# Neighbouring columns for the extra blocks of layer 0's experts, one layout of the down weights, and one order of stages for the later experts

## The chip, the cores and the metric

The kernel is one program on one core of a Trainium2 chip. Its engines are TensorE (PE in the rows: matmuls; PEld: its weight loads), VectorE (DVE), ScalarE (ACT), GpSimd (POOL) and SyncE (SP, which here only issues transfers); sixteen DMA engines move data between HBM and the on-chip memory SBUF. The metric is the device time of one execution in microseconds (us). Lower is better.

## The reference

Two layers of a diffusion backbone run over 256 latent and 256 context tokens of width 1024 in float32. Each layer has a mixer (attention and a bidirectional recurrence) and then a mixture of 16 experts, of which each token uses two:

```python
def grouped_moe(h, router_w, router_b, w_gate, w_up, w_down):
    ...  # scores, two experts of one group for each token: combine (tokens x experts)
    out = jnp.zeros_like(h)
    for e in range(N_EXPERTS):
        hid = jax.nn.silu(h @ w_gate[e]) * (h @ w_up[e])
        out = out + combine[:, e:e + 1] * (hid @ w_down[e])
    return out
```

`w_gate` and `w_up` of an expert are 1024x512, `w_down` is 512x1024: 2 MB each, 6 MB an expert, 96 MB a layer. Layer 0 sends all 512 tokens through its experts, layer 1 only the 256 latent ones, and a final normalisation ends the kernel.

## The kernel before

The change lies in the experts of layer 0, in `experts`. Layer 1 has its own code (`experts_last`), which the diff leaves alone except that it shares `part`.

For each expert the tokens routed to it are gathered into slots: a main block of 64 slots, always computed, and up to three extra blocks of 32 slots (`NX = (3, 0)`), each of which runs only if the expert has so many tokens. The test is a branch at run time (`extras`, whose conditions show as L1594 in the profile).

An expert e runs through these stages:

- `gathers(e)`: POOL fetches the tokens' rows from HBM; `xtranses(e)`: PE transposes them, ScalarE copies the result.
- `up_stage(e)`: PE multiplies with gate and up (`up0`, 8 steps over k for the main block, gate and up side by side on 64 columns of the array each). For an extra block `upx` does the same in four groups of 32 columns of the array (2 matrices x 2 halves of the 512 hidden columns), each a matmul of 256 columns. Then Silu on ScalarE (L1473, its name kept in `mark`) and the product on VectorE (`hid0`, L1474; `hidx`, L1548, for the extra blocks).
- `htranses(e)`: PE transposes the hidden values, ScalarE copies them.
- `down_stage(e)`: PE multiplies with the down weights (`down0`, `downx`).
- `out_stage(e)`: VectorE weighs the rows (L1509) and POOL adds them to HBM by an indirect transfer that accumulates (`scatter`, L1449). Scatters of different experts wait for each other.

A matmul in float32 appears as two records in the trace. In the rows `ccg` is the result of `upx`, `ccd` that of `downx`, `pgu` that of `up0`, `pdn` that of `down0`, `phd` that of the turn of the main block's hidden values.

The loop over e is written out by hand (`manual_schedule`): the engines run in the order of the code. For experts 1 to 10 one turn of the loop does up(e+1), then down(e), then the turn of the hidden values of e+1, then the output of e. For expert 0 and for experts 11 to 14 (`late`) the turn does down(e) and the output of e first, then up(e+1), then the turn of e+1. Expert 15 has only its down and output left.

Weights. `part` gives a chunk of SBUF and the source of one of an expert's three matrices. A partition p holds rows p*k_count + k of the matrix ("(p k) n"), one run of 16 KB in HBM for each partition. So for down, partition p holds the hidden columns 4p to 4p+3, and the hidden values must be put in that order: `hid0` writes its product in a turned order, and `upx` reads the weight columns four apart. Eight chunks go round. `load_expert(l, e + 2)` is called at the start of turn e, and SyncE issues its transfers; from e = 4 on they wait for `mark[e]`, the Silu of expert e (line 215). Experts 13 and 14 come in four cuts of gate and up (512 KB each). Expert 15 comes through `last_loads`: a first pair of pieces waits for `mark[13]`, two more pairs for `mark[14]`, the last pair and the down weights in four pieces for `mark2[14]`, the weighing of expert 14's output.

Behind all this in SyncE's queue stands the load of layer 1's tokens from `yd`, which waits for the last scatter.

Of the kernel before, what the change touches and what calls it, by code (L numbers as in the profile page):

```python
# [17 lines left out]
OP = mybir.AluOpType  # L18
# [4 lines left out]
KC = D // P  # L23
# [3 lines left out]
NE = 16  # L27
# [81 lines left out]
def backbone(ctx: ExitStack, tc: tile.TileContext, a: dict):  # L109
    nc = tc.nc  # L110
    pe, act, dve, pool = nc.tensor, nc.scalar, nc.vector, nc.gpsimd

    def mm(out, lhsT, rhs, start, stop):
        pe.matmul(out, lhsT, rhs, start=start, stop=stop)  # L114
# [55 lines left out]
    def wchunk(name, pl=None, dt=F32):  # L170
        if pl is None:
            pl = wpool
        else:
            return pl.tile([P, 4096], dt, name=name, tag="w")
        if wx["pool"] is not None:
            if wx["only"] is None:
                i = wx["i"] % 8
                pl = wpool if i < 4 else wx["first"] if i < 4 + wx["nf"] else wx["pool"]
                wx["i"] += 1
            else:  # L180
                pl = wx["only"]
        return pl.tile([P, 4096], dt, name=name, tag="w")
# [26 lines left out]
    def part(l, e, i, pl=None):  # L209
        n_, k = (("gate", 8), ("up", 8), ("down", 4))[i]  # L210
        t = wchunk(f"w{n_[0]}{l}_{e}", pl).rearrange("p (k n) -> p k n", k=k)
        return t, a[f"exp_w_{n_}"][l, e].rearrange("(p k) n -> p k n", k=k)

    def load(t, src, after=None, q=nc.sync):
        d = q.dma_start(t, src)
        if after:
            tc.add_manual_dep(d.ins, after, mybir.DependencyInfo(mybir.DependencyClass.Sync, mybir.DependencyReason.DATA), reason="short queue")

    def load_part(l, e, i, q, after=None):
        t, src = part(l, e, i)  # L220
        load(t, src, after, q)
        return t

    def load_expert(l, e, cuts=(), after=None):


        if not cuts:
            return [load_part(l, e, i, nc.sync, after) for i in range(3)]
        ps = [part(l, e, i) for i in range(3)]
        for lo, hi in zip((0,) + cuts, cuts + (KC,)):  # L230
            for t, src in ps[0:2]:
                load(t[:, lo:hi, :], src[:, lo:hi, :], after)
        load(*ps[2], after)
        return [t for t, _ in ps]

    def last_loads(l, e):

        ps = [part(l, e, i) for i in range(3)]

        def rows(i, lo, hi, after):  # L240
            t, src = ps[i]
            load(t[:, lo:hi, :], src[:, lo:hi, :], after)

        def steps():
            for k in range(0, KC, 2):
                after = yield
                for i in range(2):
                    rows(i, k, k + 2, after)
            for k in range(4):
                after = yield  # L250
                rows(2, 4 // 4 * k, 4 // 4 * (k + 1), after)
        g = steps()
        next(g)
        return [t for t, _ in ps], g

    ada_w = [load_ada_part(0, 0, 2 * h, 2, wchunk(f"ada{h}"), h == 3) for h in range(4)]
    csil = const.tile([P, KC, 32], F32, name="csil")
# [19 lines left out]
    with tc.tile_pool(name="spt", bufs=1, reuse_waits="tile") as sp:  # L277
# [5 lines left out]
        t = sp.tile([P, 16], F32, name="st")  # L283
        act.activation(t[:], ab[:], AF.Exp, scale=-1.0)
        s = sp.tile([P, 16], F32, name="ss")
# [26 lines left out]
    rows = {}  # L312
# [1119 lines left out]
    def experts(l, tmp):  # L1432
        r = rt_all[l]
        nt, n = r["nt"], r["n"]
        rk, ci, oi = r["rk"], r["ci"], r["oi"]
        nx = r["nx"]
        xg0, xgx, cps = (bk[n_] for n_ in ("xg0", "xgx", "cps"))
# [32 lines left out]
        def hid0(ps):  # L1470
            t = tmp.tile([P, 4, P], F32, name="hid", tag="hid", bufs=1)
            sg, h = t[64:128].rearrange("s k p -> s (k p)"), t[0:64]
            mark.append(act.activation(sg, ps[0:64, :], AF.Silu).ins.name)  # L1473
            dve.tensor_tensor(h.rearrange("s k p -> s p k"), sg.rearrange("s (p k) -> s p k", k=4),  # L1474
                              ps[64:128, :].rearrange("s (p k) -> s p k", k=4), op=OP.mult)
            return h

        def htrans0(h):
# [29 lines left out]
        def weigh(y, ps, w):  # L1508
            return dve.scalar_tensor_tensor(y, ps, w, y, op0=OP.mult, op1=OP.mult)  # L1509
# [24 lines left out]
        def upx(b, x, w):  # L1534
            for k in range(8):
                sx = x[:, b, k % 2, 32 * (k // 2):32 * (k // 2) + 32]
                for m in range(2):
                    for q in range(2):
                        wv = w[m][:, k, :].rearrange("p (c i) -> p i c", i=4)[:, 2 * q:2 * q + 2, :]
                        o = cps["cg"][64 * m + 32 * q:64 * m + 32 * q + 32, b, :].rearrange("p (i c) -> p i c", i=2)  # L1540
                        mm(o, sx, wv, k == 0, k == 7)

        def hidx():
            ps = cps["cg"]
# [56 lines left out]
        PEe, Pe = mybir.EngineType.PE, mybir.EngineType.Pool  # L1601
        W = {}
        mark = []
        mark2 = []
        oh = {}

        def onehot(e):
            if e < NE:
                oh[e] = one_hot(l, tmp, nx, rk[:, :, e])

        def infos(e):
            if e < NE:
                info[e] = slot_info(l, tmp, e, nx, oh.pop(e))
# [7 lines left out]
        def xtranses(e):  # L1621
            if e < NE:
                xt[e] = xtrans0(xg0[e % NG]), xtransx(e % NG)
# [19 lines left out]
        def out_stage(e, pd, y0, yx):  # L1643
            gs, w, _ = info[e]
            scats.clear()
            mark2.append(weigh(y0, pd, w[:, 0:1]).ins.name)
            scatter(y0, gs[:, 0:1], yd[l][:])
            for b in range(nx):
                weigh(yx[:, b, :], cps["cd"][:, b, :], w[:, 1 + b:2 + b])
            extras(Pe, e, lambda b: scatter(yx[:, b, :], gs[:, 1 + b:2 + b], ydx))  # L1650

        W[0] = load_expert(l, 0)
        with tc.manual_schedule(engines=ORDERED):
            W[1] = [load_part(l, 1, 0, nc.sync), wx["w"][0][0]]
            wx["i"] += 1
            onehot(0)
            infos(0)
            warm(ident, 8)
            r["counts"](tmp)
            gathers(0)  # L1660
            W[1].append(load_part(l, 1, 2, nc.gpsimd))
            onehot(1)
            infos(1)
            gathers(1)
            W[2] = [load_part(l, 2, i, nc.gpsimd if i < 2 else nc.sync) for i in range(3)]
            onehot(2)
            xtranses(0)
            infos(2)
            gathers(2)
            gates2()  # L1670
            onehot(3)
            up_stage(0)
            infos(3)
            xtranses(1)
            gathers(3)
            onehot(4)
            htranses(0)
            up_stage(1)
            infos(4)

            ahead_g = {0: (4,), 1: (5,), 2: (6,), 3: (7,), 4: (8,), 5: (9, 10)}
            ahead_i = {0: (5,), 1: (6,), 2: (7,), 3: (8,), 4: (9, 10)}
            for e in range(NE):
                if e + 2 < NE and e:
                    if e + 2 < NE - 1:
                        W[e + 2] = load_expert(l, e + 2, (2, 4, 6) if e + 2 >= 13 else (), mark[e] if e >= 4 else None)
                    else:
                        W[e + 2], more = last_loads(l, e + 2)
                        for _ in range(1):
                            more.send(mark[e])  # L1690
                late = e == 0 or 11 <= e < NE - 1
                if late:
                    pd = down_stage(e)
                    out_stage(e, pd, pick0(e, info[e][2]), pickx(e, info[e][2]))
                    if e == NE - 2:
                        for i in range(5):
                            try:
                                more.send(mark2[e])
                            except StopIteration:
                                break  # L1700
                xtranses(e + 2)
                for i in ahead_g.get(e, (e + 5,)):
                    gathers(i)
                for i in ahead_i.get(e, (e + 6,)):
                    onehot(i)
                    if e and i == ahead_i.get(e, (i,))[-1]:
                        up_stage(e + 1)
                        if e + 1 == NE - 2:
                            for _ in range(2):
                                more.send(mark[e + 1])  # L1710
                    infos(i)
                if late:
                    htranses(e + 1)
                    continue
                pd = down_stage(e)
                ys = pick0(e, info[e][2]), pickx(e, info[e][2])
                htranses(e + 1)
                out_stage(e, pd, *ys)
# [5 lines left out]
        with tc.If(anyv > 0, preferred_fallthrough_block=False):  # L1724
            for e in range(NE):
                ov = nc.values_load(oi[0:1, e:e + 1], min_val=0, max_val=8)
                with tc.If(ov > 0, preferred_fallthrough_block=False):
                    w = load_expert(l, e)
                    dve.memset(base[:], float(NB + 32 * nx))
                    with tc.For_i(0, ov, 1):  # L1730
# [5 lines left out]
                        ps = psb("pgu", "mm")  # L1736
                        up0(ps, x, w)
                        h = htrans0(hid0(ps))
                        ps = psb("pdn", "mm")
# [323 lines left out]
```

## Time and profile before

| | |
|---|---|
| median of 3 runs | 1153.78 us (1147.43 to 1154.68) |
| the profiled execution | 1154.09 us |
| its span from the first to the last instruction | 1152.3 us |
| mean granted TensorE clock in it | 0.936 of full speed |
| TensorE matmuls busy | 1020.5 us, 89% of the span |
| VectorE / ScalarE / GpSimd busy | 604.0 / 432.0 / 194.6 us |
| HBM read and written | 288.86 and 10.49 MB, 260 GB/s over the span |

The times of the rows are from the profiled execution and count from the start of its span. Busy time is that of an engine's own instructions; matmuls are pipelined and their ends are modelled, so the starts are the better guide to their rate. Where a row names the end of an idle time ("<-"), that is the releaser as inferred from semaphores.

### The profile page before, as it was taken

Reading aid. Unit: us, or ns where it says so; the run is one execution under the profiler, and the core shown is the slowest. Engines: PE = TensorE matmul, PEld = TensorE weight load, DVE = VectorE, ACT = ScalarE, POOL = GpSimd, SP = SyncE. Lnnn points to the kernel's source line nnn. Section 1 sums busy time; section 2 is a strip of 40 time slices with the busy share of each in tenths; the row PEclk is TensorE's granted clock in tenths of the full one; section 3 lists DMA queues with packets and bytes.
Section 4 is the critical chain, followed back from the end, with each engine's and each line's share of the span. In section 5 each row is a group of like instructions: output and inputs, shape, how many; then the busy total and the mean of one; then the engine's idle time right before and its main releaser. Section 6 shows DMA issues by size and latency. Waiting matters only on the chain. (4 is left out here: it accounts for less than half of the span.)

```text
span 1152.3 us, 15548 instructions
## 1 busy us (share of the span) xinstructions
PE 1020.5 (89%) x5791; PEld 526.3 (46%) x5791; DVE 604.0 (52%) x1363; ACT 432.0 (37%) x858; POOL 194.6 (17%) x208
## 2 busy tenths in 40 slices
PE   5999998999499998999987759997997899999993
PEld 3655555777333433333333246443676444344431
DVE  3567477787612224454443236579966144444445
ACT  3635776565311111221222054677753121122222
POOL 2100052412542211320210020102432000000000
PEclk9999999899599898999999779988997999999996
DMA  9956682103566656999995484548418699999951
GB/s 375 371 213 258 229 306 99 62 4 141 244 243 236 198 221 206 371 412 397 396 400 182 159 280 185 187 155 305 161 47 354 241 403 411 431 403 416 413 220 40
DMA packets 46252, 298.90 MB, mean 259 GB/s; under 512 B 5504, under 2 KB 8448, under 8 KB 28336
## 3 DMA queue, kind: packets, MB, share of 16 engines
q1 hardware_dynamic: 39472, 279.88, 61.5%
q0 software_dynamic: 6512, 16.87, 5.1%
q8 instruction: 74, 1.21, 0.4%
q10 hardware_dynamic: 144, 0.52, 0.1%
q14 instruction: 50, 0.41, 0.1%
HBM read 288.86 MB, written 10.49 MB: 260 GB/s over the span
## 5 line engine op out<-in xcount | busy, mean ns | idle before, releaser
L114 PE MATMUL pdn<-wd,hidT 128*64 128x512 f32 x512 | 129.6, 642 | 0.5 <-PEq L1594 0.4
L114 PE MATMUL pgu<-wu,xgT 128*64 128x512 f32 x256 | 118.4, 616 | 2.4 <-SPq L1724 2.4
L114 PE MATMUL pgu<-wg,xgT 128*64 128x512 f32 x256 | 117.5, 612 | 1.8 <-issue 1.1
L114 PE MATMUL pgu<-wu,xT 128*64 128x512 f32 x256 | 116.5, 598 | 0.0
L114 PE MATMUL pgu<-wg,xT 128*64 128x512 f32 x256 | 116.5, 598 | 0.0
L1833 DVE SCALAR_TENSOR_TENSOR xtok<-pcb,wc,xtok 128x512 f32<-128x512 f32 x64 | 47.7, 750 | 102.6 <-PE pcb L114 102.5
L1474 DVE TENSOR_TENSOR hid<-hid,pgu 64x512 f32<-64x512 f32 x16 | 17.2, 1074 | 127.3 <-ACT hid L1473 127.3
L114 PE MATMUL pproj<-hh,wps 128*128 128x512 f32 x288 | 76.9, 407 | 0.0
L1449 POOL DMA_INDIRECT yd<-xtok,sgs x24 | 38.3, 1595 | 228.7 <-DVE xtok L1509 185.8
L865 POOL TENSOR_TENSOR wo<-wf,wo 128x512 fp32r<-128x512 f32 x29 | 41.2, 1442 | 201.0 <-ACT wo L863 168.3
L114 PEld LDWEIGHTS pgu<-wg,xgT 128*64 128x64 f32 x256 | 34.6, 141 | 69.6 <-issue 68.0
L114 PEld LDWEIGHTS pdn<-wd,hidT 128*64 128x64 f32 x512 | 35.3, 145 | 64.1 <-issue 63.0
L114 PEld LDWEIGHTS pproj<-hh,wps 128*128 128x128 f32 x288 | 53.2, 188 | 19.6 <-issue 6.7
L114 PEld LDWEIGHTS pgu<-wg,xT 128*64 128x64 f32 x256 | 32.5, 136 | 61.6 <-issue 60.7
L114 PE MATMUL ccg<-wg,xxT 128*32 128x256 f32 x256 | 59.0, 633 | 0.0
L114 PE MATMUL ccg<-wu,xxT 128*32 128x256 f32 x256 | 59.0, 633 | 0.0
L1473 ACT ACTIVATE hid<-pgu 64x512 f32<-64x512 f32 x16 | 9.4, 589 | 113.3 <-PE pgu L114 113.2
L1992 POOL TENSOR_TENSOR fin<-xtok,fin 128x512 f32<-128x512 f32 x2 | 2.5, 1278 | 254.9 <-DVE xtok L1833 254.9
L1786 ACT ACTIVATE hid<-pgu 64x512 f32<-64x512 f32 x16 | 9.4, 589 | 94.5 <-PE pgu L114 94.5
L1548 DVE TENSOR_TENSOR hix<-hix,ccg 64x768 f32<-64x768 f32 x16 | 15.1, 942 | 54.4 <-ACT hix L1547 54.4
L814 ACT ACTIVATE Pm<-psc,mx,qy 128x512 f32<-128x512 f32 (+1 forms) x48 | 33.5, 702 | 20.5 <-DVE mx L808 20.3
L516 DVE TENSOR_TENSOR wps<-win,wps 128x512 fp32r<-128x512 f32 x48 | 32.6, 686 | 15.3 <-ACT wps L515 14.8
(442 smaller groups left out, 2123.8 us busy)
## 6 DMA issues: line engine op xcount, KB each, us to landing
wd<-exp_w_down_dram SPq DMA_DIRECT2D x30, 2048.0 KB
wu<-exp_w_up_dram SPq DMA_DIRECT2D x27, 2048.0 KB
wg<-exp_w_gate_dram SPq DMA_DIRECT2D x27, 2048.0 KB
xtok<-ada_w_dram SPq DMA_DIRECT2D x7, 2048.0 KB
win<-w_in_dram SPq DMA_DIRECT2D x6, 2048.0 KB
adac<-ada_w_dram SPq DMA_DIRECT2D x5, 2048.0 KB
xtok<-ada_w_dram SPq DMA_DIRECT2D x8, 1024.0 KB
adac<-ada_w_dram SPq DMA_DIRECT2D x8, 1024.0 KB
```

What stands on the lines that cost most here:

```text
L114: pe.matmul(out, lhsT, rhs, start=start, stop=stop)
L516: dve.tensor_tensor(wl, wv, wh.bitcast(F32), op=OP.subtract)
L814: act.activation(ps[h], sc_[i][h], AF.Exp, bias=mx[:, h:h + 1], scale=qr[:, ti, j, h:h + 1], accum_out=sm[:, h:h + 1])
L865: pool.tensor_tensor(lo, w, hi.bitcast(F32), op=OP.subtract)
L1449: st = pool.indirect_dma_start(out=dst, out_offset=bass.IndirectOffsetOnAxis(ap=idx, axis=0), in_=y, in_offset=None, bounds_check=dst.shap ...
L1473: mark.append(act.activation(sg, ps[0:64, :], AF.Silu).ins.name)
L1474: dve.tensor_tensor(h.rearrange("s k p -> s p k"), sg.rearrange("s (p k) -> s p k", k=4), ps[64:128, :].rearrange("s (p k) -> s p k", k=4) ...
L1548: dve.tensor_tensor(t[0:64].rearrange("s b k p -> s b (k p)"), sg, ps[64:128, 0:nx], op=OP.mult)
L1786: act.activation(sg, ps[0:64, :], AF.Silu)
L1833: dve.scalar_tensor_tensor(x, cb, wc[:, t, e:e + 1], x, op0=OP.mult, op1=OP.add)
L1992: (dve if q else pool).tensor_tensor(fin["t"][:, 1 + t, cs], x, fin["t"][:, 0, cs], op=OP.mult)
```

## The change

It does three things.

The down weights of layer 0 are loaded as "(k p) n": partition p holds rows p, 128+p, 256+p and 384+p, so four runs of 4 KB for each partition and no longer one of 16 KB. With that the hidden values can stay in their natural order: `hid0` writes its product without turning, and `upx` reads 256 neighbouring columns of gate and up. Its four groups, their order and their number of columns stay.

The weights of expert 15 are loaded by `load_expert` like those of 13 and 14: four cuts of gate and up and one transfer of 2 MB for down, all waiting for `mark[13]`. `last_loads` and `mark2` go.

`late` is only expert 0. Experts 11 to 14 now take the order of experts 1 to 10.

```diff
@@ part
         t = wchunk(f"w{n_[0]}{l}_{e}", pl).rearrange("p (k n) -> p k n", k=k)
-        return t, a[f"exp_w_{n_}"][l, e].rearrange("(p k) n -> p k n", k=k)
+
+        return t, a[f"exp_w_{n_}"][l, e].rearrange("(k p) n -> p k n" if i == 2 and l == 0 else "(p k) n -> p k n", k=k)
@@ last_loads
-    def last_loads(l, e):
-
-        ps = [part(l, e, i) for i in range(3)]
...
-        def steps():
-            for k in range(0, KC, 2):
-                after = yield
-                for i in range(2):
-                    rows(i, k, k + 2, after)
-            for k in range(4):
-                after = yield
-                rows(2, 4 // 4 * k, 4 // 4 * (k + 1), after)
...
@@ hid0
-            dve.tensor_tensor(h.rearrange("s k p -> s p k"), sg.rearrange("s (p k) -> s p k", k=4),
-                              ps[64:128, :].rearrange("s (p k) -> s p k", k=4), op=OP.mult)
+            dve.tensor_tensor(h.rearrange("s k p -> s (k p)"), sg, ps[64:128, :], op=OP.mult)
@@ upx
-                        wv = w[m][:, k, :].rearrange("p (c i) -> p i c", i=4)[:, 2 * q:2 * q + 2, :]
-                        o = cps["cg"][64 * m + 32 * q:64 * m + 32 * q + 32, b, :].rearrange("p (i c) -> p i c", i=2)
-                        mm(o, sx, wv, k == 0, k == 7)
+                        mm(cps["cg"][64 * m + 32 * q:64 * m + 32 * q + 32, b, :], sx, w[m][:, k, 256 * q:256 * q + 256], k == 0, k == 7)
@@ out_stage
-            mark2.append(weigh(y0, pd, w[:, 0:1]).ins.name)
+            weigh(y0, pd, w[:, 0:1])
@@ the loop over the experts
                 if e + 2 < NE and e:
-                    if e + 2 < NE - 1:
-                        W[e + 2] = load_expert(l, e + 2, (2, 4, 6) if e + 2 >= 13 else (), mark[e] if e >= 4 else None)
-                    else:
-                        W[e + 2], more = last_loads(l, e + 2)
-                        for _ in range(1):
-                            more.send(mark[e])
-                late = e == 0 or 11 <= e < NE - 1
-                if late:
+                    W[e + 2] = load_expert(l, e + 2, (2, 4, 6) if e + 2 >= 13 else (), mark[e] if e >= 4 else None)
+                if e == 0:
                     pd = down_stage(e)
                     out_stage(e, pd, pick0(e, info[e][2]), pickx(e, info[e][2]))
-                    if e == NE - 2:
-                        for i in range(5):
-                            try:
-                                more.send(mark2[e])
...
                         up_stage(e + 1)
-                        if e + 1 == NE - 2:
-                            for _ in range(2):
-                                more.send(mark[e + 1])
                     infos(i)
-                if late:
+                if e == 0:
                     htranses(e + 1)
                     continue
                 pd = down_stage(e)
```

## Rows read from the trace of the kernel before

**Rows 1.** The page's 40 slices of 28.8 us, tenths busy or granted.

```profile
PE   5999998999499998999987759997997899999993
PEclk9999999899599898999999779988997999999996
DMA  9956682103566656999995484548418699999951
```

**Rows 2.** Windows by stage: experts 0 to 3, 4 to 10, 11 to 15 of layer 0.

```profile
core 0: us, PE busy (x) PEld busy (x) DVE busy (x) ACT busy (x) POOL busy (x), PEclk, DMA share, GB/s
...
318.70:448.50 129.80, 120.55 (x957) 47.29 (x954) 33.63 (x86) 18.06 (x38) 34.02 (x38) 0.93 0.62 230
448.50:566.00 117.50, 108.49 (x766) 44.14 (x764) 56.33 (x138) 26.65 (x58) 24.18 (x18) 1.00 0.94 365
566.00:661.30 95.30, 77.12 (x338) 28.42 (x336) 30.44 (x55) 15.75 (x31) 10.45 (x7) 0.89 0.72 266
```

**Rows 3.** Windows by expert, from one up stage's start to the next: 6, 11, 13, 14, 15.

```profile
482.36:497.20 14.84, 13.57 (x85) 5.48 (x84) 7.84 (x21) 3.75 (x9) 3.23 (x3) 1.00 1.01 406
...
566.08:585.25 19.17, 16.66 (x85) 6.28 (x84) 9.48 (x18) 3.58 (x8) 4.24 (x3) 1.00 1.02 394
...
603.08:621.92 18.84, 14.72 (x70) 5.77 (x70) 5.67 (x10) 4.13 (x9) 1.84 (x2) 0.91 0.71 265
621.92:638.06 16.14, 13.41 (x58) 5.22 (x58) 4.37 (x7) 2.13 (x4) 0.00 (x0) 0.89 0.41 137
638.06:661.24 23.18, 17.41 (x58) 5.67 (x58) 5.23 (x10) 2.24 (x4) 1.55 (x1) 0.78 0.44 148
```

**Rows 4.** Windows, instructions of `ccg` alone (no POOL column): experts 0 to 3, 4 to 10.

```profile
318.70:448.50 129.80, 51.66 (x448) 17.09 (x448) 3.82 (x4) 3.21 (x4) 0.93 0.62 230
448.50:566.00 117.50, 7.45 (x64) 2.30 (x64) 6.57 (x7) 5.54 (x7) 1.00 0.94 365
```

**Rows 5.** Timeline of PE (start us, us, ...), extra blocks: `ccg` five steps, `ccd` merged.

```profile
333.40 0.64 PE L114 MATMUL ccg<-wg,xxT 128*32 128x256 f32 x2
...
335.21 0.64 PE L114 MATMUL ccg<-wg,xxT 128*32 128x256 f32 x2
...
371.94 5.39 PE L114 MATMUL ccd<-wd,hixT 128*32 128x256 f32 x96
```

**Rows 6.** Timeline of SyncE's queue: requests for expert 15's weights.

```profile
610.83 0.33 SPq L215 DMA_DIRECT2D wg<-exp_w_gate_dram  x1
...
629.66 0.33 SPq L215 DMA_DIRECT2D wg<-exp_w_gate_dram  x1
...
640.10 2.93 SPq L215 DMA_DIRECT2D wd<-exp_w_down_dram  x4
```

**Rows 7.** DMA view of 464 to 605 us: queue, packets, MB, share.

```profile
q1 hardware_dynamic: 5104, 51.67, 88.2%
```

**Rows 8.** Windows with 16 KB rows only, then with 4 KB rows only.

```profile
404.00:408.00 4.00, 3.07 (x40) 1.21 (x37) 1.98 (x6) 0.00 (x0) 1.62 (x1) 1.00 1.01 426
...
632.00:636.00 4.00, 4.00 (x14) 1.24 (x14) 1.45 (x4) 0.48 (x1) 0.00 (x0) 0.63 0.99 388
```

**Rows 9.** Groups by line (busy us, mean ns, idle before): two VectorE products of 64x512.

```profile
L1816 DVE TENSOR_TENSOR hl<-y,hl 64x512 fp32r<-64x512 f32 x32 | 22.0, 686 | 13.7 <-ACT hl L1815 13.2
...
L1474 DVE TENSOR_TENSOR hid<-hid,pgu 64x512 f32<-64x512 f32 x16 | 17.2, 1074 | 127.3 <-ACT hid L1473 127.3
```

**Rows 10.** Timeline of PE: down(10), turn(11), down(11).

```profile
573.57 3.65 PE L114 MATMUL pdn<-wd,hidT 128*64 128x512 f32 x16 [0.40 <-PEq L1594]
577.87 0.46 PE L1481 MATMUL phd<-ident,hid 64*128 64x64 f32 x4 [0.65 <-DVE xtok L1506]
...
578.84 3.65 PE L114 MATMUL pdn<-wd,hidT 128*64 128x512 f32 x16
```

**Rows 11.** Timeline of POOL: scatters of experts 10, 11 and 15.

```profile
579.27 1.58 POOL L1449 DMA_INDIRECT yd<-xtok,sgs  x1 [8.08 <-DVE xtok L1509]
588.43 1.55 POOL L1449 DMA_INDIRECT yd<-xtok,sgs  x1 [7.58 <-DMA yd<-xtok,sgs]
...
662.32 1.55 POOL L1449 DMA_INDIRECT yd<-xtok,sgs  x1 [22.29 <-DVE xtok L1509]
```

More of the change, by code (lines that the diff above doesn't have):

```diff
@@ L234, in load_expert @@
         return [t for t, _ in ps]
-    def last_loads(l, e):
-        ps = [part(l, e, i) for i in range(3)]
-        def rows(i, lo, hi, after):
-            t, src = ps[i]
-            load(t[:, lo:hi, :], src[:, lo:hi, :], after)
-        def steps():
-            for k in range(0, KC, 2):
-                after = yield
-                for i in range(2):
-                    rows(i, k, k + 2, after)
-            for k in range(4):
-                after = yield
-                rows(2, 4 // 4 * k, 4 // 4 * (k + 1), after)
-        g = steps()
-        next(g)
-        return [t for t, _ in ps], g
     ada_w = [load_ada_part(0, 0, 2 * h, 2, wchunk(f"ada{h}"), h == 3) for h in range(4)]
@@ L1603, in experts @@
         mark = []
-        mark2 = []
         oh = {}
@@ L1684, in experts @@
                 if e + 2 < NE and e:
-                    if e + 2 < NE - 1:
-                        W[e + 2] = load_expert(l, e + 2, (2, 4, 6) if e + 2 >= 13 else (), mark[e] if e >= 4 else None)
-                    else:
-                        W[e + 2], more = last_loads(l, e + 2)
-                        for _ in range(1):
-                            more.send(mark[e])
-                late = e == 0 or 11 <= e < NE - 1
-                if late:
+                    W[e + 2] = load_expert(l, e + 2, (2, 4, 6) if e + 2 >= 13 else (), mark[e] if e >= 4 else None)
+                if e == 0:
                     pd = down_stage(e)
                     out_stage(e, pd, pick0(e, info[e][2]), pickx(e, info[e][2]))
-                    if e == NE - 2:
-                        for i in range(5):
-                            try:
-                                more.send(mark2[e])
-                            except StopIteration:
-                                break
                 xtranses(e + 2)
```

## The prediction, made before the change was run

> **What bounds the kernel now.** I read the page first, for where the engines are full. Each digit of [rows 1] is a slice of 28.8 us. From slice 11 to slice 23 (317 to 662 us) runs the stage that the diff touches: the sixteen experts of layer 0. The clock digits there are mostly 9, and the DMA digit goes from 5 or 6 to 9 and falls back near the end. So the stage has parts with different limits, and I cut it into three with the view of windows [rows 2]. In experts 0 to 3 TensorE (PE) is busy 120.55 of 129.80 us while DMA has a share of 0.62: PE sets the time. In experts 4 to 10 PE is busy 108.49 of 117.50 us and DMA 0.94: both are nearly full. In experts 11 to 15 neither is: 77.12 of 95.30 us and 0.72, with a granted clock of 0.89. The same view by single experts [rows 3] shows what a plain expert costs when PE goes through without a pause: 14.84 us at clock 1.00, DMA 1.01. Experts 11, 13, 14 and 15 take 19.17, 18.84, 16.14 and 23.18 us, and DMA drops to 0.71, 0.41 and 0.44 in the last three.
>
> Two things are to be explained: the 51.66 us of PE in experts 0 to 3 that go to the extra blocks' up matmuls [rows 4], and the slack at the end.
>
> **The change, part by part.**
>
> *A and B, neighbouring columns.* The extra blocks that really run are counted by their matmul records: one block has 8 k x 2 matrices x 2 halves, each two records, so 64. [Rows 4] have 448 records in experts 0 to 3 and 64 after: seven blocks and one. Four records run side by side. In [rows 5] four such steps take from 333.40 to 335.21, 0.45 us a step, for 256 columns that lie four floats apart. The extra blocks' down matmuls have the same shape, 128x256 on 32 columns of the array, but neighbouring columns: 96 records, 24 steps, in 5.39 us, 0.225 us a step [rows 5]. Nothing else differs that could cost the factor of two: same size, four groups side by side, output in PSUM in one run in both. The new code reads neighbouring columns. The bounds are no gain (0.46 us a step, 7.38 us a block by [rows 4]) and the down step: 16 x 0.225 = 3.59 us a block. I take the latter, its row being the same form. A: 7 x (7.38 - 3.59) = 26.5 us. B: 7.45 - 3.59 = 3.9 us. In experts 0 to 3 DMA has 38% to spare, so A is not eaten there.
>
> [...]
>
> *C, the order of experts 11 to 14 and the loads of expert 15.* Before, each of experts 11 to 14 ran down(e), then up(e+1), then the turn of the hidden values, so PE waited for ScalarE and VectorE in between; the diff gives them the order of experts 4 to 10. Expert 15's weights were requested in pieces that waited for later and later marks: a first pair at 610.83, two pairs at 629.66, the last pair and the down matrix by 640.10 [rows 6]. Now all wait for one mark, expert 13's Silu. Before, from the start of up(11) at 566.08 to the last scatter at 662.32 [rows 11] it is 96.2 us. After: four periods of 14.85 us to the start of up(15), 59.4; up(15) 7.3 (16 steps of a pair of matmuls, where down's 8 steps take 3.65 us, [rows 10]) and 0.4 to the next stage, the gap before down in [rows 10]: 67.1. Then down(14), the turn, down(15), which before occurs once in this sequence, for experts 10 and 11: 573.57, 577.87, 578.84 and 3.65 us, 8.9 us in all [rows 10]. And its scatters show what is late next: expert 11's scatter, ready about 1 us after its down, waited for that of expert 10 to land and left at 588.43, 14.9 us after 573.57 [rows 11]. That was with DMA full. With DMA idle the last scatter needs no such wait (661.3 to 662.32), and 8.9 + 1.1 = 10.0 is the other bound. I take 12.5, since expert 15's weights will just have landed by then. So 67.1 + 12.5 = 79.6: C = 16.6 us (14.2 to 19.1). On POOL nothing else is passed: the last gather belongs to expert 10's turn, and the scatters keep their order.
>
> *D, what DMA takes back.* Before, DMA in the window of expert 13 is busy 0.71 x 18.84 = 13.4 us [rows 3], so all that was requested by then, up to the first pair of expert 15, had landed at about 616.5. That queue was full from expert 6 at the latest [rows 3], so it moves by A alone: 590.0. Then come 3.1 MB of gate and up, at 388 to 426 GB/s [rows 8] 7.4 to 8.1 us: 598 or so. The down matrices of layer 0 now come in rows of 4 KB and no longer 16 KB; the nearest rows are the windows of [rows 8]: 426 GB/s with 16 KB, 388 with 4 KB, so 4.9 and 5.4 us for 2.1 MB, at most 0.5 us for each of the nine (experts 6 to 14) in that queue, 4.3 us; I take 2.7. The last gate and up rows are then there at 601. PE would want them at 566.08 - 30.4 + 59.4 + 7.3 - 1.8 = 600.6 (the last two of eight k take the 1.8). That is about even. By the rate of a full queue (51.67 MB in 141 us [rows 7], 17.2 us an expert against PE's 14.85) PE would be some 5 us late. D = 3 us, from 0 to 5.
>
> *Costed at nothing.* The product of gate and up on VectorE, 1.07 us with its turned write [rows 9], becomes a plain one; the nearest plain row of 64x512 is 0.69 us. It is hidden under down(e), 3.65 us, in the common order; without that cover it is 0.4 us an expert, in our favour. The first experts' 4 KB rows hide in the DMA share of 0.62. Expert 15's nine requests are issued by SyncE in one go; behind them in its queue stands only the load of layer 1's tokens, which waits for the last scatter anyway.
>
> **The sum.** 26.5 + 3.9 + 16.6 - 3 = 44.0 us. The profiled execution took 1154.09 us (span 1152.3 and 1.8 around it), 0.3 above the median of the runs shown. 1154.1 - 44.0 = 1110.1, so 1110. All that follows in layer 1 hangs on the last scatter and moves as a whole.
>
> **The rivals.**
>
> *1. The stride was not what cost.* Then A and B are nothing, PE is later and so DMA early by comparison (D = 0), and C alone is left: 1154.1 - 16.6 = 1137.5. The price would then belong to something that the change keeps, two weight matrices read in turn, say, where down reads one. Against it stands the 0.225 us of down, which also streams four different pieces side by side. [...]
>
> *2. The end is not won.* Loads that are no longer held back keep DMA full, and scatters land late: each waits for the one before, and VectorE's result buffers come round after three experts. PE is held only when a landing takes longer than the period of 14.85 us; expert 10's, with DMA full, took from 579.27 to 588.43, 9.2 us [rows 11]. At 19 us the four experts would lose 4 x 4.2 = 16.8 us, all of C: 1154.1 - 30.4 = 1123.7.
>
> [...]
>
> **The numbers.** My forecast 0.75, rival 2 0.13, rival 1 0.07, rival 3 0.02, and 0.03 that two things fail and it ends within 1%. The likeliest case by itself spans 1101 to 1118: with C at its best and D nothing it is 1104.6, with C at its least and D of 5 it is 1114.5, and half of the 7.2 us by which the runs of before differ goes on either side. The range reaches into rival 2: 1100 to 1127. About 1% is what a measurement of this kernel can tell from no change; faster by more has 0.75 + 0.13 + 0.07 = 0.95, within it 0.03, slower 0.02.
>
> **What will show it.** The up matmuls of the extra blocks at 0.22 us a step and about 29 us in all instead of 59: A and B. If they stay at 0.45, the prediction is wrong by 27 us. Experts 11 to 14 at 14.9 to 17 us each with DMA at 0.95 or more until expert 15's weights are in: C and D. A last scatter near 618, held by the one before it: the end of C. [...] From the last scatter on, the distance to the end should be as before, 490 us.

## The result, and the profile after

The changed kernel takes 1108.8 us (median; 1102.0 to 1110.9) against 1153.2 us of the kernel before: a ratio of 0.961, 95% interval 0.956 to 0.967. A second measurement on another occasion (E11 below) gave 1111.4 us and 0.967 (0.964 to 0.970). 1110 had been forecast.

The profiled execution took 1107.5 us, its span is 1105.6. The page's 40 slices are 27.6 us each now; the layer 0 experts lie in slices 11 to 22, counted from 0. The clock and DMA rows answer to [rows 1]:

```profile
PEclk9999999899669989999998799998997999999996
DMA  9947674011866876999997565558156799999941
```

In slices 11 to 15 the DMA digits are 6, 6, 8, 7 and 6, where before had 6, 6, 6, 5 and 6. Then come five slices at 9 in both, and the last two of the stage are 7 and 5 for 5 and 4. The windows by stage answer to [rows 2] (columns as there):

```profile
317.50:420.80 103.30, 93.77 (x956) 43.25 (x954) 34.13 (x86) 18.20 (x38) 35.57 (x38) 0.93 0.79 291
420.80:534.54 113.74, 104.74 (x765) 43.79 (x764) 55.13 (x139) 26.69 (x58) 25.45 (x19) 1.00 0.95 364
534.54:617.40 82.86, 71.62 (x337) 26.53 (x336) 31.02 (x58) 15.68 (x31) 9.72 (x7) 0.96 0.85 324
```

For the comparison the last stretch of before is taken to its last scatter as well, 566.08 to 662.32, 96.24 us. Between the two profiled executions the gains are 129.86 - 103.33 = 26.5 us in experts 0 to 3 (between exact starts), 117.53 - 113.74 = 3.8 us in experts 4 to 10, and 96.24 - 82.86 = 13.4 us from the start of up(11) to the last scatter: 43.7 us. The remaining 3.0 us of 46.7 lie outside: the part ahead of the stage is 1.2 us shorter and the distance from the last scatter to the end 488.2 for 490.0 us, neither touched by the diff.

The same view with `ccg` alone, for the first two stretches, answers to [rows 4]:

```profile
317.50:420.80 103.30, 25.00 (x448) 14.15 (x448) 3.82 (x4) 3.21 (x4) 0.93 0.79 291
420.80:534.54 113.74, 3.66 (x64) 1.98 (x64) 6.69 (x7) 5.54 (x7) 1.00 0.95 364
```

The first and the last of a block's sixteen steps, from the timeline of TensorE, answer to [rows 5]:

```profile
491.34 0.41 PE L114 MATMUL ccg<-wg,xxT 128*32 128x256 f32 x2
...
494.60 0.39 PE L114 MATMUL ccg<-wg,xxT 128*32 128x256 f32 x2
```

The same 448 and 64 records take 28.66 us instead of 59.11. Fifteen steps from 491.34 to 494.60 are 0.217 us each. Experts 11 to 15, one line each, answer to [rows 3]:

```profile
534.54:548.99 14.45, 13.09 (x69) 5.21 (x69) 5.51 (x10) 3.59 (x8) 3.51 (x3) 1.00 1.01 398
548.99:564.65 15.66, 14.28 (x70) 5.44 (x69) 5.51 (x10) 3.59 (x8) 1.55 (x1) 1.00 1.02 390
564.65:578.82 14.17, 13.08 (x69) 5.05 (x68) 5.51 (x10) 3.69 (x8) 1.55 (x1) 1.00 1.03 398
578.82:592.84 14.02, 12.00 (x60) 4.27 (x59) 5.13 (x10) 2.10 (x5) 0.52 (x1) 0.98 1.03 397
592.84:617.40 24.56, 19.18 (x75) 6.57 (x74) 9.36 (x19) 2.72 (x5) 2.58 (x2) 0.87 0.45 155
```

Four experts at 14.0 to 15.7 us with the clock at 0.98 or 1.00 and DMA full; then one of 24.56 us with 0.87. What that one consists of is in the timeline of TensorE (the rest of down(13), down(14), the turn and down(15); in brackets the idle time ahead and what ended it):

```profile
590.17 1.08 PE L114 MATMUL pdn<-wd,hidT 128*64 128x512 f32 x4 [1.18 <-issue]
...
605.11 5.35 PE L114 MATMUL pdn<-wd,hidT 128*64 128x512 f32 x16 [2.65 <-PEq L1572]
611.10 0.46 PE L1461 MATMUL phd<-ident,hid 64*128 64x64 f32 x4 [0.63 <-PEq L1572]
...
612.07 3.65 PE L114 MATMUL pdn<-wd,hidT 128*64 128x512 f32 x16
```

Here PEq is TensorE's own sequencer, and "issue" stands for idle time in which the engine waited for nothing that the profile shows. The scatters of experts 12 to 15 are in the timeline of POOL:

```profile
577.24 1.55 POOL L1430 DMA_INDIRECT yd<-xtok,sgs  x1 [13.01 <-DVE xtok L1489]
592.32 1.55 POOL L1430 DMA_INDIRECT yd<-xtok,sgs  x1 [13.53 <-DVE xtok L1489]
611.53 1.55 POOL L1430 DMA_INDIRECT yd<-xtok,sgs  x1 [17.66 <-DVE xtok L1489]
617.40 1.55 POOL L1430 DMA_INDIRECT yd<-xtok,sgs  x1 [4.32 <-DVE xtok L1489]
```

All four scatters waited for VectorE's result, none for a landing. up(15) ended at 602.47, but down(14) began only at 605.11: 2.65 us in which the profile names the sequencer's branch (line 1572, over the extra blocks) and nothing that TensorE lacked. And down(14) then took 5.35 us, at a granted clock of 0.68, where down(15) took 3.65 at 1.00. Neither was in the forecast. up(15) itself took 9.63 us where an undisturbed one takes 7.1; its first half, as a window:

```profile
592.84:598.00 5.16, 4.88 (x16) 1.57 (x17) 0.38 (x1) 0.48 (x1) 1.03 (x1) 0.74 1.03 389
```

Its first three steps take 0.85 us and more each, for 0.43 of the later ones: about 1.3 of the 2.5 us is the lower clock (0.74 in this half, 0.50 over those three steps, 592.84 to 595.45), right behind a pause of 1.18 us in down(13) and one of 0.55 ahead of the turn. The rest is pieces that come late and a stop of 0.28 us.

### The profile page after: what moved, and what is told of

It is laid out like the page before. It is cut to its first block, busy times and chain, and to the rows that moved or that the text cites. A ratio compares the mean times of both kernels' runs of the same rounds, so it can differ in the third digit from the quotient of the medians.

```text
span 1105.6 us, 15540 instructions
## 1 busy us (share of the span) xinstructions
PE 984.8 (89%) x5791; PEld 520.2 (47%) x5791; DVE 600.5 (54%) x1363; ACT 432.3 (39%) x858; POOL 195.7 (18%) x208
## 5 line engine op out<-in xcount | busy, mean ns | idle before, releaser
L114 PE MATMUL pdn<-wd,hidT 128*64 128x512 f32 x512 | 124.3, 619 | 5.3 <-PEq L1572 4.0
L1455 DVE TENSOR_TENSOR hid<-hid,pgu 64x512 f32<-64x512 f32 x16 | 11.0, 690 | 126.2 <-ACT hid L1454 126.2
L114 PE MATMUL pproj<-hT,wps 128*128 128x512 f32 x144 | 39.8, 397 | 0.0
L114 PEld LDWEIGHTS pgu<-wu,xgT 128*64 128x64 f32 x256 | 34.8, 142 | 6.9 <-issue 5.2
L114 PE MATMUL pwa<-wo,mh 128*128 128x512 f32 x128 | 36.3, 407 | 1.6 <-POOL wo L846 0.9
## 6 DMA issues: line engine op xcount, KB each, us to landing
wd<-exp_w_down_dram SPq DMA_DIRECT2D x31, 2048.0 KB, 14.2
```

The source lines that it names most:

```text
L1455: dve.tensor_tensor(h.rearrange("s k p -> s (k p)"), sg, ps[64:128, :], op=OP.mult)
```

## The experiments

Each run also has a run of the kernel before on the same chip. "Last stretch" is always from the start of up(11) to the last scatter.

**E1 and E2, the two halves alone.** E1 has the layout of the down weights, the plain product and the neighbouring columns, with the old order and the old loads of expert 15; E2 the new order and loads with the old columns.

```diff
 E1: against before
-   wv = w[m][:, k, :].rearrange("p (c i) -> p i c", i=4)[:, 2 * q:2 * q + 2, :]
+   w[m][:, k, 256 * q:256 * q + 256]
...
 E2: against before
-   W[e + 2], more = last_loads(l, e + 2)
+   W[e + 2] = load_expert(l, e + 2, (2, 4, 6) if e + 2 >= 13 else (), mark[e] if e >= 4 else None)
-   late = e == 0 or 11 <= e < NE - 1
+   late = e == 0
```

> The layout and the neighbouring columns alone; the order of experts 11 to 14 and the staggered loads of expert 15 are those of before. If A and B are what the prediction says, the extra blocks' up matmuls fall from 59 to about 29 us and the time by 30.4 us, and by up to 1.6 us more where the plain product shortens the four late turns by 0.4 us each: 1121 to 1124 us. If the columns cost nothing (rival 1), it stays at 1152 to 1154. If DMA takes the gain back in experts 4 to 10, it lies in between, near 1135.

> The order of stages and the loads of expert 15 alone; layout, product and columns are those of before. If C is 16.6 us and DMA does not bind, PE being later, it gives 1136 to 1138 us. If the end is won only because the columns brought PE forward, it stays near 1153. If the two parts share their gain, the gains of this one and of the columns alone add up to clearly more than the 44 us of both together; if they are separate, to 44 to 48.

E1: 1126.6 us, 0.980 (0.975 to 0.985). E2: 1132.1 us, 0.983 (0.979 to 0.988). Against 1152.8 on that chip that is 26.2 and 20.7 us. E1 ends 2.6 us above what was expected of it, E2 4 us below. Together they would make 46.9; the whole change has 40.0 (E11) to 44.4. The windows of experts 11 to 15 in E2:

```profile
561.50:575.90 14.40, 13.03 (x69) 5.18 (x68) 5.70 (x10) 3.54 (x8) 2.79 (x3) 1.00 1.01 398
575.90:590.20 14.30, 13.12 (x70) 5.23 (x69) 5.71 (x10) 3.61 (x8) 2.99 (x2) 1.00 1.03 404
590.20:604.40 14.20, 13.11 (x71) 5.08 (x70) 5.70 (x10) 3.72 (x8) 1.55 (x1) 1.00 1.04 406
604.40:617.30 12.90, 11.69 (x60) 4.01 (x59) 5.06 (x9) 1.90 (x5) 0.24 (x1) 1.00 1.02 393
617.30:638.06 20.76, 15.86 (x76) 5.74 (x74) 10.09 (x20) 2.77 (x6) 2.86 (x2) 1.00 0.41 137
```

The last stretch is 76.6 us, 19.7 less than before, with the clock at 1.00 in all five windows. Expert 15 took 20.76 us although its weights were there in time; in the timeline its up stage has one stop:

```profile
622.40 0.59 PE L114 MATMUL pgu<-wg,xgT 128*64 128x512 f32 x1 [1.88 <-issue]
```

In E1 the stretch is 95.9 us and has won nothing from DMA's head start. One reason is in its timeline: an idle TensorE ahead of up(14), waiting for nothing that the profile shows either:

```profile
596.76 0.99 PE L114 MATMUL pgu<-wg,xgT 128*64 128x512 f32 x1 [3.60 <-issue]
```

**E3, the order taken back.** The kernel after, with the old order for experts 11 to 14 (down, next up, turn), the loads left as in after.

```diff
-   if e == 0:            # twice in the loop
+   if e == 0 or 11 <= e < NE - 1:
```

> The changed kernel with the old order (down first) for experts 11 to 14, its free loads of expert 15 kept. It divides C between order and loads. From the rows of before an old turn lasts 17.8 to 19.2 us, less 0.4 for the plain product, so up(15) starts about 12 us later than in the changed kernel, but without waiting for weights, and down(14) and its scatter are over by then: the last scatter comes only 2 to 4 us later, 1111 to 1113 us. If the order is what C consists of, it loses all of C: 1122 to 1125.

1121.7 us, 0.973 (0.968 to 0.978): the time that the rival gave, and not the 1111 to 1113 expected. The last stretch is 91.1 us, 8.2 more than in after, although DMA is full (1.01 to 1.03) up to the start of up(14). So in these profiles the order is worth more than half of the 13.4 us that after won there, and the free loads the rest (E1 to E3: 95.9 to 91.1, 4.8). Here too one gap of this kind stands in it, ahead of up(14):

```profile
598.47 1.01 PE L114 MATMUL pgu<-wg,xgT 128*64 128x512 f32 x1 [3.89 <-issue]
```

**E4, the early request taken back.** The kernel after, but expert 15's weights are requested only behind expert 14's Silu.

> The changed kernel, but all loads of expert 15 wait for the Silu of expert 14 and no longer of 13, some 14 us later. If DMA is full until expert 14's down weights are in (589.7 us in the trace of the changed kernel, 4 us after that Silu), little is lost: 1109 to 1111 us. If the early request is what C consists of, the end moves by most of those 14 us: 1118 to 1123.

1111.7 us, 0.966 (0.961 to 0.970), just above what was expected; last stretch 81.9 for 82.9. Asking one expert earlier bought nothing that shows in the new order. What E3 has over E1 then comes, most likely, from all nine transfers going off together; that was not tried by itself.

**E5, what in the old reads cost.** The extra blocks read their columns at three distances. This leaves out that they are the right columns, so the tokens served by these blocks get other values, and only the steps of these matmuls are read.

```diff
-   w[m][:, k, 256 * q:256 * q + 256]
+   b == 0: row.rearrange("p (c i) -> p i c", i=2)[:, q, :]
+   b == 1: row.rearrange("p (j i c) -> p i j c", i=2, c=128)[:, q, :, :]
+   b == 2: row[:, 0:384].rearrange("p (c i) -> p i c", i=3)[:, q:q + 2, :]
```

> The kernel after, but the extra blocks' up matmuls read their 256 columns in three ways: block 0 (experts 0, 1, 2, 3, 8) two floats apart; block 1 (experts 0, 3) in two runs of 128 neighbouring columns that lie 256 apart; block 2 (expert 0) in two runs of 128 columns three floats apart. What is changed is which hidden columns the extra blocks compute, so the part of the output that comes through them has other values; only the step of these matmuls (four records side by side) is read, not the total. [...] Theory 2, any distance between columns costs the factor of two: block 0 and block 2 at 0.45 us a step (7.3 us a block), block 1 at 0.22. Theory 3, the two-part pattern of the old reads cost, not the distance: block 0 at 0.22, blocks 1 and 2 at 0.45.

The timeline of expert 0's three blocks, the first and the sixteenth step of each:

```profile
328.27 0.42 PE L114 MATMUL ccg<-wg,xxT 128*32 128x256 f32 x2
...
331.69 0.39 PE L114 MATMUL ccg<-wg,xxT 128*32 128x256 f32 x2
331.92 0.38 PE L114 MATMUL ccg<-wg,xxT 128*32 128x256 f32 x2
...
335.15 0.39 PE L114 MATMUL ccg<-wg,xxT 128*32 128x256 f32 x2
335.37 0.51 PE L114 MATMUL ccg<-wg,xxT 128*32 128x256 f32 x2
...
340.54 0.51 PE L114 MATMUL ccg<-wg,xxT 128*32 128x256 f32 x1
```

Block 0, two floats apart: (331.69 - 328.27) / 15 = 0.228 us. Block 1, two runs of neighbours: 0.215. Block 2, three floats apart: (340.54 - 335.37) / 15 = 0.345. Neither theory 2 (0.45 for block 2, and for block 0) nor theory 3 (0.45 for block 1) fits. With the 0.45 us at four floats [rows 5] the step follows the distance: if it costs 0.45 us times a quarter of the distance in floats, but not less than 0.216, distances of two, three and four floats make 0.225, 0.34 and 0.45. A distance of two floats is nearly free (0.228 for 0.216), three and four are not (0.345 and 0.45); the two-run pattern costs nothing (0.215). What it is in the distance that costs, these steps do not show.

**E8, the branch hints taken out.** Ahead of the branches over the extra blocks' up matmuls both kernels set a hint for TensorE that marks the skip as likely (`LikelyTaken` in the diff). E8 is the kernel after without the hints.

```diff
 def skip_hint(label, b):
-    if b < nx:
-        tc.mark_branch_hint_location(f"{label}_{b}", "LikelyTaken", engines=[PEe])
+    pass
```

> The kernel after without the hints that stand ahead of the branches over the extra blocks' up matmuls. Theory: the gaps of TensorE behind a branch with nothing to wait for (2.65 us before down(14), 3.46 us in the routing stage ahead of expert 3) are fetches of its instructions, each with one 16 KB packet of the instruction queue inside it; with no hint the jump over the extra blocks pays one in most of the eleven experts without extra blocks, 1 to 3.5 us each, 11 to 38 us in all, most of it in experts 4 to 15: 1120 to 1146 us, with an instruction packet inside each gap. Rival: the gaps come from the branch waiting on its count or on weights and have nothing to do with fetches: 1107 to 1111 us, and no new gaps.

1127.1 us, 0.978 (0.974 to 0.981): 18 us more than after and 16 more than E11, as the theory had it. The windows of E8's three stretches (to up(4), to up(11), to the last scatter):

```profile
316.92:413.80 96.88, 91.34 (x959) 42.71 (x956) 34.26 (x86) 18.14 (x38) 35.67 (x38) 0.96 0.81 299
413.80:552.40 138.60, 111.69 (x766) 45.58 (x765) 55.30 (x138) 27.11 (x58) 25.78 (x20) 0.94 0.90 335
552.40:637.40 85.00, 70.38 (x337) 26.68 (x336) 30.87 (x58) 15.68 (x31) 8.86 (x6) 0.96 0.77 271
```

One of its new gaps in the timeline of TensorE:

```profile
543.50 0.57 PE L114 MATMUL pslot<-vals,oh 128*128 128x5 bf16 x16 [2.62 <-PEq L1571]
```

The instruction queue in the DMA view of just this gap, 540.88 to 543.50 (packets, MB, share of the time of 16 engines):

```profile
q8 instruction: 1, 0.02, 2.1%
```

Experts 4 to 10 take 138.6 us for 113.7. From up(4) to the last scatter there are twelve gaps over 0.8 us, 29.7 us in all, and in ten of them a 16 KB packet of the instruction queue (in after it has 73, 1.20 MB) starts within the gap or up to 0.7 us ahead of it and runs into it. What they share is closer than that: all twelve end 1.5 to 1.9 us after the end of such a packet. The gap of the kernel after ahead of down(14) looks the same: its packet runs from 602.50 to 603.45, 1.7 us before down(14) starts. This is the instruction queue from 602.47 to 605.11:

```profile
q8 instruction: 1, 0.02, 2.3%
```

Two more stops of after, 1.18 us within down(13) and 3.46 us ahead of expert 3's slot matmuls, end 1.3 and 1.4 us after a packet. That these idle times are fetches of TensorE's instructions is the author's reading of the queue's name and of these times; the profile ties no packet to a stop. The queues were not full in all of them: DMA's share is 1.04 in the 3.46 us, but 0.27 in the gap ahead of down(14) and 0.33 in E1's 3.60 us, whose packet ends 1.4 us before up(14) starts.

One expert is longer with the hint, which had not been asked about: expert 3, two of whose extra blocks do run, against what the hint says, takes 30.1 us in after and 24.0 in E8. Its window in after:

```profile
390.70:420.80 30.10, 25.27 (x246) 11.18 (x244) 8.12 (x20) 3.92 (x9) 4.50 (x4) 0.89 0.72 252
```

and in E8:

```profile
389.80:413.80 24.00, 22.41 (x247) 10.47 (x246) 8.13 (x20) 3.76 (x9) 4.72 (x4) 1.00 0.73 268
```

Without the hint a gap of 3.46 us ahead of its slot matmuls is gone and the clock stays at 1.00. That the hint costs wherever blocks run is not shown: experts 0 to 2 run five of the seven blocks behind the same hints and take 23.3, 27.0 and 22.9 us in after, 23.2, 26.9 and 22.8 in E8. Hints for the later experts alone would be a version to try; it wasn't run.

**E9, no load for expert 15.** It computes with expert 14's weights, so the tokens that expert 15 serves get other values, and only the stage is read.

```diff
-   W[15] = load_expert(l, 15, (2, 4, 6), mark[13])
+   W[15] = W[14]
```

> The kernel after, but expert 15 of layer 0 computes with expert 14's weights and its own are not loaded (left out: expert 15's weights, so the tokens that it serves get other values). This takes 6.3 MB out of the end of the queue; only the stretch from the start of up(11) to the last scatter is read, 82.86 us in the kernel after and 76.6 in the run with the new order alone. If what DMA takes back at the end is the late pieces of expert 15, up(15) goes from 9.63 to 7.1 to 7.4 us, the clock stays high in down(14), and the stretch falls by 4 to 6 us to 77 to 79. If it is the fetch ahead of down(14) alone, up(15) shortens but the gap of 2.65 us stays: 80 to 81. If it is neither, 82 to 83.

The last stretch is 75.3 us, below even the 77 to 79 of the first theory. The window of expert 15 up to the last scatter:

```profile
597.60:615.40 17.80, 15.22 (x76) 5.27 (x74) 9.45 (x19) 2.77 (x6) 2.87 (x3) 1.00 0.16 22
```

down(14) in the timeline of TensorE:

```profile
604.99 3.65 PE L114 MATMUL pdn<-wd,hidT 128*64 128x512 f32 x16 [0.31 <-PEq L1572]
```

and the instruction queue in the DMA view of that window:

```profile
q8 instruction: 4, 0.07, 1.8%
```

up(15) takes 7.1 us, the gap ahead of down(14) is 0.31, down(14) takes 3.65 at clock 1.00. Four instruction packets pass in that window and none stops TensorE. One of them starts at 601.92, 4.33 us into up(15); in after the one ahead of down(14) starts at 602.50, when up(15) is already over. So the late pieces, the stop and the lower clock of expert 15 are all gone with the load of its weights, in this one execution. How the load brings the stop about is not shown: when the packet was requested is not in the profile, and DMA's share had fallen to 0.27 in the gap.

**E10, no branches in the last experts.** The kernel after without TensorE's branches over the extra blocks of experts 11 to 15.

```diff
-   extras(PEe, e, ...)          # up_stage and down_stage
+   if e < 11: extras(PEe, e, ...)
```

> The kernel after without TensorE's branches over the extra blocks of experts 11 to 15 (with these inputs none of them is taken, so the same blocks are computed). If TensorE's stops there (2.65 us before down(14), 1.18 inside down(13)) are fetches behind those branches, both go, and the last scatter comes 2 to 4 us earlier: 1104.5 to 1107. If they come from the full DMA queue alone, whatever the code, gaps of that size stand elsewhere in the same stretch and it is even: 1107.5 to 1110. The late pieces of expert 15 hold up(15) as before in both.

1108.7 us, 0.964 (0.961 to 0.967), beside 1111.4 for after on the same chip (E11): 2.6 less, with overlapping intervals, and inside the 1107.5 to 1110 of the rival, so not settled by the times. The trace is clearer: the last stretch is 77.4 us for E11's 82.8 (2.3 of these 5.4 us are lost again ahead of up(0), which the edit does not touch), both gaps (1.18 us within down(13) and 2.65) are gone, and now up(15) is what waits, piece by piece. From 589.1 to 615.5 no instruction packet passes at all. The skipped blocks' code went with the branches, so E10 does not tell which of the two the gaps hang on. The window of expert 15:

```profile
594.80:617.10 22.30, 18.34 (x74) 5.55 (x74) 10.94 (x22) 2.36 (x5) 3.11 (x3) 0.99 0.58 202
```

and in the timeline of TensorE up(15) and the start of down(14):

```profile
594.84 1.04 PE L114 MATMUL pgu<-wg,xgT 128*64 128x512 f32 x2 [0.38 <-DMA wg<-exp_w_gate_dram]
598.58 0.64 PE L114 MATMUL pgu<-wu,xgT 128*64 128x512 f32 x1 [0.20 <-DMA wu<-exp_w_up_dram]
...
605.55 4.02 PE L114 MATMUL pdn<-wd,hidT 128*64 128x512 f32 x15
```

TensorE gets to up(15) 55.1 us after up(11) (58.3 in after) and is held there by gate and up pieces one after the other, 11.3 us in all. down(14) follows without a pause, its first matmul between the last of up(15), and the window has clock 0.99.

**E6 and E12, the 4 KB rows.** The kernel after, but the down weights of experts 4 to 7 and 9 to 15 in rows of 16 KB, with the turned product. E12 is the same kernel once more, E11 the kernel after beside it.

```diff
-   "(k p) n -> p k n" if i == 2 and l == 0
+   "(k p) n -> p k n" if i == 2 and l == 0 and (e < 4 or e == 8)
```

> The kernel after, but the down matrices of experts 4 to 7 and 9 to 15, whose extra blocks don't run, are laid out as before: rows of 16 KB in place of 4 KB, with the turned write of the hidden product. This measures the term of the 4 KB rows in what DMA takes back, taken as 2.7 us and at most 4.3. If it is as taken: the last gate and up rows of expert 15 land 2 to 3 us earlier than 600.5, the last scatter comes 2 to 3 us earlier, 1105.5 to 1107 us, ratio to after 0.997 or so. If the rows cost nothing, 1108 to 1109.5 as after; if only the turned write shows, 1109 to 1112.

> The kernel after once more, beside the next run on the same chip: 1105 to 1111 us.

> The kernel with 16 KB rows for the down matrices of experts 4 to 7 and 9 to 15 once more, beside the kernel after. In its first profile the last pieces of expert 15 landed no earlier than in the kernel after (601.3 against 600.5) and the stage was only 1.0 us shorter, though its time was 6 us lower. If the rows matter, it is 2 to 6 us below the kernel after here too; if that was a difference between runs, the two are within 1.5 us.

E6: 1102.8 us, 0.957 (0.954 to 0.959), below the 1105.5 to 1107 expected. E12: 1108.9, 0.964 (0.960 to 0.967), with E11 at 1111.4, 0.967 (0.964 to 0.970). The sign is the same both times, but side by side it is 2.5 us with overlapping intervals. Last stretches: 80.1 and 81.7 us with 16 KB rows, 82.9 and 82.8 with 4 KB rows. One window of 60 us with a full queue, first in E11 (4 KB rows; last column GB/s):

```profile
530.00:590.00 60.00, 54.40 (x290) 22.30 (x289) 22.60 (x45) 14.86 (x30) 7.34 (x5) 1.00 1.03 395
```

and in E12 (16 KB rows):

```profile
530.00:590.00 60.00, 55.07 (x302) 21.64 (x298) 23.41 (x45) 14.62 (x29) 7.34 (x5) 1.00 1.02 398
```

395 GB/s against 398; in the same window after has 397 and E6 399. E2 and before, with all down weights in 16 KB rows, have 398 and 396 from 540 to 600. So the rates differ by less than 1%, which on the 57 MB of nine experts is an estimated 1 us. The 2.7 us between the last stretches of E6 and after are not all rows: E6 has the clock at 1.00 up to its last scatter, after had not. Whether the kernel with long rows beats after stays open.

**E7, a version that might beat both.** The kernel after with the old order for expert 14 alone, so that down(14) and its scatter fall into the time in which TensorE waits for expert 15's pieces.

> The kernel after, with the old order (down, then the next up, then the turn) for expert 14 alone. Theory: at the end TensorE waits for expert 15's last pieces anyway, so down(14) and its scatter fit into that wait, and only down(15) is left behind up(15): the last scatter 4 to 6 us earlier than 617.4, near 612, and 1102 to 1105 us. Rival: the turn of 15 stands exposed again (3 to 4 us between up(15) and down(15)) and the next gap of TensorE with nothing to wait for falls in the same place, so it is even: 1107 to 1111.

1108.2 us, 0.963 (0.961 to 0.966): no better than after, as the rival said. down(14) is earlier, but the turn of 15 is exposed, as the timeline of TensorE shows (down(14), then the turn):

```profile
598.13 1.08 PE L114 MATMUL pdn<-wd,hidT 128*64 128x512 f32 x3 [1.67 <-issue]
608.37 0.46 PE L1461 MATMUL phd<-ident,hid 64*128 64x64 f32 x4 [1.40 <-DVE hid L1455]
609.88 0.58 PE L1534 MATMUL phx<-ident,hix 64*128 64x64 f32 x6 [1.06 <-DVE hix L1526]
```

1.40 and 1.06 us of turn come back, and a stop of 1.67 us stands within down(14).

## Why the prediction was right, and where its steps were not

**A, 26.5 us: right for the matmuls, generous for the stage.** The extra blocks' up matmuls lost 51.66 - 25.00 = 26.66 us, and E5 shows that it was the distance between the columns. That experts 0 to 3 became shorter by 26.5 us too is partly this pair of profiles: in ten executions with neighbouring columns and hints they take 103.0 to 107.9 us, median 106.5, in two with the old columns (before and E2) 129.9 and 126.6, so about 22 us is typical. With E11, at 106.7 us, the matmuls of `ccg` are again 25.00; the rest of TensorE's time is 96.52 - 25.00 = 71.5 us, where after has 68.8, at a granted clock of 0.91 for 0.93. What the prediction took from DMA's share as room was room. Of the 3.4 us by which this stage of E11 is longer than that of after, 2.7 are these other TensorE instructions, at the lower mean clock.

**B, 3.9 us: right.** 7.45 - 3.66 = 3.8, and the stretch shows 3.8. This is where TensorE and DMA are both nearly full, and TensorE still set the time.

**C, 16.6 us: the mechanism right, the size too small.** E2 gives 19.7, above the range of 14.2 to 19.1. Two terms were off. The period of 14.85 us was that of expert 6 [rows 3], which also carries the slot matmuls for a later expert (0.50 us from their start to down's, with 0.29 us ahead of them where down alone has 0.40: 0.39 us a period); experts 11 to 14 don't, and expert 14 has no tokens left to turn. So the four periods of E2 sum to 55.8 and not 59.4. And the tail from the start of down(14) was taken as 12.5 since the last scatter would wait for the landing of the one before. It didn't: all scatters of after waited for VectorE, and E2 needs 11.2 us from the end of up(15), the gap included, where 12.9 had been put. Against that up(15) takes 9.6 us and not 7.3, nearly all of it in the stop of 1.88 us, which ends 1.5 us after an instruction packet, as in E8. 3.6 + 1.7 - 2.3 = 3.0.

**D, 3 us: too small, and in the wrong place.** The last stretch of after is 6.3 us longer than E2's, where 5 was the most. The forecast of the queue was good: the last gate and up piece was put at 601 and lands at 600.5 in the trace. It put the loss into up(15) waiting for these pieces. In fact up(15) ends at 602.47, and the prediction's own sum without D ends it at 602.4: late pieces cost some 1 us there and 1.25 in up(12) (its first gate matmuls run alone and wait for the up weights), the lower clock 1.3, and all that only ate what the shorter periods had won. What made the end late came behind: the stop ahead of down(14), 2.65 us where 0.4 was put, and 1.7 us more in down(14) at a granted clock of 0.68 (0.50 from 606 to 609).

E9 shows that all of it in expert 15 goes with the load; E10, that the gap goes with the branches and the blocks behind them. So the step that failed is the assumption that TensorE, once its data are there, runs on: the price of the loads was looked for in late weights alone, and the instruction queue (73 packets, 1.20 MB in all of after) had no term. The lower clock, 1.3 and 1.7 us here, did not come in every run: E6 and E7 have stops of 1.67 to 2.23 us in this stretch and stay at 1.00. The 4 KB rows, 2.7 of the 3 us, are nearer 1 by the rates of E6 and E12.

C and D erred by 3.0 and 3.3 us in opposite directions, so the sum was right to 0.3 us for the profiled stage, 43.7 against 44.0. That is luck as far as these two terms go. B and the matmuls of A are not luck; that the first stage gave all of A in this pair of profiles is. In E11 the three stages are 23.1, 3.5 and 13.5 us shorter than before, some 40 in all.

**Costed at nothing: held.** The product is now 690 ns where it was 1074 [rows 9], and in the common order nothing waits for it; TensorE does where the turn is exposed, as in E7.

**The rivals.** Rival 1 (the distance is not the cause) falls by E1 and E5. Rival 2 (the scatters hold TensorE) falls by the four POOL rows of after. Rival 3, to which 0.02 went, stood for a fall of the granted clock that leaves the kernel slower: the clock fell in one expert, to 0.87 in the window of expert 15, with 0.98 and 1.00 in the other four, and the kernel is 4% faster. The distance from the last scatter to the end stayed, 488 for 490 us.

## What to carry to other kernels

When a matmul takes twice as long as its neighbour of the same form, compare how their operands lie in SBUF: here fp32 columns two apart were nearly free (0.228 us a step for 0.216), and three or four apart cost in proportion (0.345 and 0.45). Take a stage's period from an expert that issues just what the later ones issue, and count its instructions first. Where TensorE stands idle with its data there, look when the last instruction packet landed: here the stops ended 1.3 to 1.9 us after one, and without the hints for the skips there were twelve from up(4) to the last scatter (E8, 29.7 us).

## What the runs showed of the hardware that was not expected

- An idle TensorE that "waits for nothing" stood behind an instruction packet: stops of 1.1 to 5.5 us in after and E8, each ending 1.3 to 1.9 us after a 16 KB packet of the instruction queue; not only behind a branch (1.80 us within down(13) of E11, 1.67 within down(14) of E7). DMA's share in such a stop can be 0.27 (after) or 0.33 (E1); yet in E9, without expert 15's load, four packets passed and cost nothing.
- Hints are worth 16 to 18 us in this kernel (1127.1 us without, 1111.4 and 1108.8 with), although expert 3, whose blocks do run, is some 6 us longer with them (30.1 for 24.0).
- The granted clock fell behind single pauses of 1.18 and 2.65 us in after (0.50 over the first 2.6 us of up(15), and from 606 to 609 in down(14)), but not behind the 1.88 us in E2, the 1.74 to 2.23 us in E6 or the 1.80 and 1.67 us in E7. In E10, where TensorE was held by piece after piece but not idle for longer than 0.4 us from the start of up(15) to the end of down(14), it was 0.99 over the window. Why it differs was not tried by itself.
